# q and k as features by tokens, and a score order by row groups, in a two-layer decoder trunk

## The chip, the cores and the metric

The kernel runs on one core of a Trainium2 chip. Its time is the device time of one execution in microseconds. Before the change three runs gave a median of 648.08 us (648.01 to 648.24). The profile is one more execution of its own.

## The reference

Two layers for 256 tokens of width 1024, in float32. Layer 0 has block-sparse attention, which with one block of 256 keys is plain causal attention; layer 1 has differential attention, in which every head's 128 features are two halves of 64 with a softmax map each. Cut to what matters:

```python
for i in range(DEPTH):
    mod = (c_act @ ada_w[i] + ada_b[i])[:, None, :]          # c_act = silu(c)
    sh_a, sc_a, g_a, sh_f, sc_f, g_f = jnp.split(mod, 6, axis=-1)
    h = rms_norm(x, norm_g[i, 0]) * (1.0 + sc_a) + sh_a
    y = moba_attention(h, ...) if i % 2 == 0 else diff_attention(h, ...)
    x = x + g_a * rms_norm(y, norm_g[i, 1])
    h = rms_norm(x, norm_g[i, 2]) * (1.0 + sc_f) + sh_f
    x = x + g_f * rms_norm(swiglu(h, ffn_w_in[i], ffn_w_out[i]), norm_g[i, 3])

# attention: q, k, v = split(h @ w_qkv, 3); 8 heads
s = q k^T * scale + bias[head, bucket(q_pos - k_pos)];  s = where(rel >= 0, s, -1e30)
# layer 0: p = softmax(s);  o = p v
# layer 1: p[c] = softmax(s[c]) for the halves c = 0, 1;  o = (p[0] - lam * p[1]) v, then a norm per head
y = o @ w_o
```

## The kernel before

The 256 tokens are two tiles of 128. Every large product is written as three products in a faster 32-bit type (`R`): both operands are split into a high part (a copy by ScalarE, line 483 for weights, line 513 for activations) and a low part (a subtraction by VectorE, lines 484 and 514), and `mm` (line 485 on) adds high x high, high x low and low x high into one PSUM bank. In `mm` the activations `h` are the stationary operand, 128 features by 128 tokens, and a row block of weights with 512 columns is the moving one, so that a result has tokens on partitions and 512 features beside each other.

q and k are wanted with features on partitions. `qk_T` (line 574) therefore copies such a result to SBUF with ScalarE, turns it with four TensorE transposes (`pqk`) and copies it again. The scores (`softmax`, line 587) then take `qT` as stationary and `kT` as moving operand, head by head. In layer 1 each half of a head is a step of its own, with partitions 0 to 63 or 64 to 127 of both; the steps of the two halves stand in TensorE's queue where the plan puts them. A score of plain float32 counts as two products in the trace.

The relative-position bias is a table times a one-hot matrix (`build_bias`, line 318): a product with 8 rows, one per head, a copy to `bd` on 8 partitions, a store that repeats it 23 times in DRAM (`toep`), and loads with shifted rows (`load_bias`).

`first_block` is the start: norm of x, transposes of it (`ph`, `xT`), the adaLN vectors for the first feature chunk by one-column products on TensorE (`ada_first`, `pg` at line 419) and for the later chunks by VectorE multiply-adds (line 362) with sums over partitions by TensorE (line 374). Each chunk's shift and scale go to `hm`, `hq`, and to the projections of q and k. Ahead of it ten products of ones (`warm`, line 302), whose result nobody reads, run on TensorE.

The order of the work is not that of the code. Every step is an `op` with a cost, its buffers and a priority from the table `PRIORITIES`; `Schedule.run` plays the steps through with these costs, with PSUM and SBUF slots (`a` and `bc` have four PSUM banks each), and so writes the five queues (TensorE, VectorE, ScalarE, GpSimd, SyncE for transfers). On the chip each queue runs in that order.

Of the kernel before, what the change touches and what calls it, by code (L numbers as in the profile page):

```python
# [12 lines left out]
F = mybir.dt.float32  # L13
# [50 lines left out]
class Schedule:  # L64
# [35 lines left out]
    def run(self):  # L100
# [20 lines left out]
        order, act = [], "silu"  # L121
# [18 lines left out]
        while len(order) < len(ops):  # L140
            soon, moved = [], False
            for e in ENGINES:
# [25 lines left out]
                elif e == "PE":  # L168
# [6 lines left out]
                    cold -= d  # L175
# [52 lines left out]
def ld(nbytes):  # L228
    return nbytes / 360e3
# [3 lines left out]
def trunk_kernel(ctx: ExitStack, tc: tile.TileContext, x, c, rel_bias, ada_w, ada_b, norm_g, moba_w_qkv, moba_w_o,  # L233
# [51 lines left out]
    op("POOL", 0.05, lambda: nc.gpsimd.memset(mh.t, -0.5), w=[mh])  # L285
    op("DVE", 0.3, lambda: nc.vector.tensor_reduce(sel[:, 0], ident[:].rearrange("p (a b) -> p b a", a=4), AX.X, OP.add),
# [31 lines left out]
    def build_bias():  # L318
        oh = Buf("oh", "kT1", [NB + 1, NTOEP])
        tab = keep("tab", [NB + 1, H])  # L320
        bd = Buf("bd", "PT1", [H, NTOEP])
# [4 lines left out]
        op("PE", 0.65, lambda: nc.tensor.matmul(pb[:H, :NTOEP], tab.t[:], oh.t[:], start=True, stop=True), r=[tab, oh], w=[pb])  # L326
        op("DVE", 0.47, lambda: nc.vector.tensor_copy(bd.t, pb[:H, :NTOEP]), r=[pb], w=[bd])
        op("SP", 0.8, lambda: nc.sync.dma_start(toep.t, bd.t[:, None, :].to_broadcast([H, NCOPY, NTOEP])), r=[bd], w=[toep])

    def load_bias(g):  # L330
# [7 lines left out]
        for h in range(4):  # L338
            op("SP", ld(128 * 1024), lambda h=h: f(h), r=[toep], w=[(bt, K(h))])
# [58 lines left out]
    def ada_first(k0, n):  # L398
# [7 lines left out]
        for kc in range(0, KC, q):  # L406
# [3 lines left out]
            for j in range(2):  # L410
# [76 lines left out]
    def mm(ps, h, k, W, n, first, last, main=True):  # L487
# [6 lines left out]
        for q in range(3):  # L494
            op("PE", cost, lambda q=q: f(q), r=[(h, K(10 + k if q == 2 else k))] + [(b, K(1 if q == 1 else 0)) for b, _ in W],
               w=list(ps), main=main, name="mm" + W[0][0].name)

# [78 lines left out]
    def qk_T(st, l, t, g, w, ps):  # L576

        if t == 0:
# [7 lines left out]
            dst[:, :, t * 128:t * 128 + 128], p.t[:].rearrange("p (h q) -> p h q", h=4), AF.Copy), r=[p], w=[(dst, K(t))])  # L586

    def softmax(st, l, t, g):
# [358 lines left out]
```

## Time and profile before

| | us |
|---|---|
| median of the timed runs | 648.08 (648.01 to 648.24) |
| the profiled execution | 645.48 |
| its span, first to last instruction | 643.7 |
| TensorE busy | 627.5 (97%) |
| VectorE busy | 475.0 (74%) |
| ScalarE busy | 372.5 (58%) |

A product's duration in the trace is the time from its start to its end in a pipeline, longer than the distance to the next one: the mean of a 512-column product is some 390 to 410 ns, while 28 in a row take 6.35 us. What a product costs in a queue is therefore read from the time of a dense row of them. The chain of waits and the merged timeline give such rows.

### The profile page before, as it was taken

Reading aid. Unit: us, or ns where it says so; the run is one execution under the profiler, and the core shown is the slowest. Engines: PE = TensorE matmul, PEld = TensorE weight load, DVE = VectorE, ACT = ScalarE, POOL = GpSimd, SP = SyncE. Lnnn points to the kernel's source line nnn. Section 1 sums busy time; section 2 is a strip of 40 time slices with the busy share of each in tenths; the row PEclk is TensorE's granted clock in tenths of the full one; section 3 lists DMA queues with packets and bytes.
Section 4 is the critical chain, followed back from the end, with each engine's and each line's share of the span. In section 5 each row is a group of like instructions: output and inputs, shape, how many; then the busy total and the mean of one; then the engine's idle time right before and its main releaser. Section 6 shows DMA issues by size and latency. Waiting matters only on the chain.

```text
span 643.7 us, 8416 instructions
## 1 busy us (share of the span) xinstructions
PE 627.5 (97%) x2955; PEld 515.0 (80%) x2955; DVE 475.0 (74%) x602; ACT 372.5 (58%) x628; POOL 30.0 (5%) x66
## 2 busy tenths in 40 slices
PE   7899999999999999999989999999999999999996
PEld 6787878887888888888877777787788888888884
DVE  3798699987689969659885889898655657574633
ACT  6477697589364625345596777848655344453621
POOL 1000000031000000000021000211200000000001
PEclk9999999999999999999999999999999999999999
DMA  9999999997889987758965868472575587665301
GB/s 291 360 363 319 300 378 381 347 292 249 301 285 353 363 313 270 233 174 293 351 233 194 291 218 271 133 229 72 190 262 163 187 272 224 250 199 180 128 1 66
DMA packets 72487, 160.58 MB, mean 249 GB/s; under 512 B 5491, under 2 KB 22516, under 8 KB 72444
## 3 DMA queue, kind: packets, MB, share of 16 engines
q1 hardware_dynamic: 72252, 159.96, 73.0%
q8 instruction: 23, 0.38, 0.2%
q14 instruction: 20, 0.16, 0.1%
q10 hardware_dynamic: 192, 0.08, 0.0%
HBM read 158.69 MB, written 1.33 MB: 249 GB/s over the span
## 4 chain that ended last, share of the span: by engine, by line
PE 85%; DMA 5%; DVE 3%; ACT 3%; POOL 2%; issue 1%; SPq 1%; DVEq 0%; POOLq 0%; ACTq 0%
PE pf L492 19%; PE pg L492 16%; PE pu L492 16%; PE pq L492 10%; PE pv L492 6%; PE po L492 5%; PE pgu L492 3%; DMA bias<-toep 3%; PE ps L603 2%; PE pa L296 1%; PE po L649 1%; PE ph L296 1%; ACT hm L508 1%; DMA toep<-bd 1%; PE pg L419 1%
## 5 line engine op out<-in xcount | busy, mean ns | idle before, releaser
L492 PE MATMUL pg<-s_i,h 128*128 128x512 f32 x480 | 188.3, 392 | 0.0
L492 PE MATMUL pu<-s_i,h 128*128 128x512 f32 x480 | 187.1, 390 | 0.0
L484 DVE TENSOR_TENSOR s_i<-w_i,s_i 128x1024 fp32r<-128x1024 f32 (+1 forms) x96 | 107.0, 1133 | 50.7 <-ACT s_i L483 49.7
L492 PE MATMUL pf<-s_u,a 128*128 128x512 f32 x528 | 137.4, 392 | 0.0
L483 ACT ACTIVATE s_i<-w_i 128x1024 fp32r<-128x1024 f32 (+1 forms) x96 | 93.1, 989 | 73.3 <-PE pu L492 48.8
L492 PEld LDWEIGHTS pf<-s_u,a 128*128 128x128 f32 x528 | 97.9, 188 | 20.4 <-ACT s_u L483 0.4
L492 PEld LDWEIGHTS pg<-s_i,h 128*128 128x128 f32 x480 | 90.1, 188 | 18.8 <-DVE s_i L484 0.3
L492 PEld LDWEIGHTS pu<-s_i,h 128*128 128x128 f32 x480 | 90.1, 188 | 18.4
L362 DVE SCALAR_TENSOR_TENSOR acc<-aw,cact,acc 128x1024 f32<-128x1024 f32 x70 | 89.3, 1277 | 2.2 <-DMA aw<-in_ada_w_dram 1.8
L483 ACT ACTIVATE s_u<-w_u 128x1024 fp32r<-128x1024 f32 x44 | 46.4, 1059 | 58.3 <-PE pu L492 28.8
L484 DVE TENSOR_TENSOR s_u<-w_u,s_u 128x1024 fp32r<-128x1024 f32 x44 | 53.6, 1221 | 30.2 <-ACT s_u L483 29.8
L492 PE MATMUL po<-s_o,o 128*128 128x512 f32 x192 | 49.8, 399 | 0.0
L492 PE MATMUL pq<-s_q,h 128*128 128x512 f32 x192 | 47.7, 397 | 1.8 <-ACT h L513 1.8
L492 PEld LDWEIGHTS pq<-s_q,h 128*128 128x128 f32 x192 | 35.0, 188 | 10.5 <-ACT h L513 2.5
L484 DVE TENSOR_TENSOR s_q<-w_q,s_q 128x1024 fp32r<-128x1024 f32 x32 | 38.5, 1220 | 5.9 <-ACT s_q L483 5.6
L492 PEld LDWEIGHTS po<-s_o,o 128*128 128x128 f32 x192 | 34.9, 188 | 6.8 <-DVE o L665 0.4
L492 PE MATMUL pq<-s_q,hq 128*128 128x512 f32 x144 | 37.0, 408 | 2.5 <-ACT hq L513 2.5
L483 ACT ACTIVATE s_q<-w_q 128x1024 fp32r<-128x1024 f32 x32 | 33.3, 1054 | 4.8 <-PE pq L492 2.0
L492 PEld LDWEIGHTS pq<-s_q,hq 128*128 128x128 f32 x144 | 27.5, 195 | 9.2 <-ACT hq L513 3.0
L471 POOL TENSOR_SCALAR ms<-ss 128x1 f32<-128x1 f32 x16 | 7.3, 459 | 504.7 <-ACT z L542 497.9
L611 ACT ACTIVATE sx<-sx,mx 128x128 f32<-128x128 f32 (+1 forms) x48 | 21.3, 445 | 10.6 <-DVE mx L609 10.6
L492 PE MATMUL pgu<-s_i,h 128*128 128x512 f32 x96 | 26.1, 392 | 0.0
(141 smaller groups left out, 755.7 us busy)
## 6 DMA issues: line engine op xcount, KB each, us to landing
aw<-in_ada_w_dram SPq DMA_DIRECT2D x80, 512.0 KB
w_i<-in_ffn_w_in_dram SPq DMA_DIRECT2D x80, 512.0 KB
w_u<-in_ffn_w_out_dram SPq DMA_DIRECT2D x44, 512.0 KB
aw<-in_ada_w_dram SPq DMA_DIRECT2D x32, 256.0 KB
w_q<-in_moba_w_qkv_dram SPq DMA_DIRECT2D x16, 512.0 KB
w_q<-in_diff_w_qkv_dram SPq DMA_DIRECT2D x16, 512.0 KB
w_q0v<-in_moba_w_qkv_dram SPq DMA_DIRECT2D x8, 512.0 KB
w_o<-in_moba_w_o_dram SPq DMA_DIRECT2D x8, 512.0 KB
```

Of the source, the lines that this page charges most:

```text
L296: nc.tensor.transpose(dst[:, o:o + n], a, ident[:n, :n])
L362: op("DVE", tt(n) + 0.065, lambda: nc.vector.scalar_tensor_tensor(a.t, w(), cact[:, kc:kc + 1], a.t, op0=OP.mult, op1=OP.add), r=[cact, w. ...
L419: nc.tensor.matmul(pg[:, n * j + b:n * j + b + 1], w[:, e, j, b * 128:b * 128 + 128], cact[:, kc + e:kc + e + 1], start=kc + e + j + b == ...
L471: op("POOL", 0.16, lambda: nc.gpsimd.tensor_scalar(ms.t, m0.t[:], 1.0 / n, EPS, op0=OP.mult, op1=OP.add), r=[m0], w=[ms])
L483: op("ACT", ac(2 * n), lambda: nc.scalar.activation(b[:, 0], w.t[:], AF.Copy), r=[w], w=[(b, K(0))], name="hi" + name)
L484: op("DVE", tt(2 * n), lambda: nc.vector.tensor_sub(b[:, 1], w.t[:], b[:, 0].bitcast(F)), r=[w, (b, K(0))], w=[(b, K(1))], name="lo" + name)
L492: nc.tensor.matmul(p[:, :n], a, b[:, 1 if q == 1 else 0, s], start=first and q == 0, stop=last and q == 2)
L508: op("ACT", ac(128, 2, fps), lambda i=i, k=k: nc.scalar.activation(m[:, i], src[2](i), AF.Identity, bias=sh[:, k:k + 1], scale=G[:, k:k + 1]),
L603: nc.tensor.matmul(p[:, i * nk:i * nk + nk], qT[rows, h0 + i, t * 128:t * 128 + 128], kT[rows, h0 + i, 0:nk], start=True, stop=True)
L611: op("ACT", ac(nk, 2), lambda i=i, sx=sx, mx=mx, su=su: nc.scalar.activation(sx[:, i], sx[:, i], AF.Exp, bias=mx[:, i:i + 1], accum_out=su ...
L649: nc.tensor.matmul(p[:, i * 128:i * 128 + 128], a, b, start=kt == 0, stop=kt == t)
```

## The change

- In layer 0, and for heads 4 to 7 of layer 1, q and k are computed by `mmT` with the weights (128 x 128) as stationary and `h` of both tiles (256 columns) as moving operand. The result has features on partitions, and `qk_F` copies it once. For this the two tiles' activations lie in one SBUF tile `hh`. Heads 0 to 3 of layer 1 keep the old way.
- In layer 1 the scores of both halves are one step, in which the halves alternate.
- The bias product has 128 rows (16 copies of the 8 heads), and two stores take the table from 128 partitions.
- 22 instead of ten `warm` products, one more behind each of the four adaLN steps of the first chunk and five behind the last.
- A one-column silu right at the start, so that its table is loaded there.
- The planner's start without a loaded table, some of its costs, and the whole table of priorities are new, and so are all five queues.

```diff
-        order, act = [], "silu"
+        order, act = [], None
...
+    scr = keep("scr", [128, 1])
+    op("ACT", 0.2, lambda: nc.scalar.activation(scr.t, mh[:, 0:1], AF.Silu), r=[mh], w=[scr], act="silu")
...
-    for _ in range(10):
-        op("PE", 0.227, lambda: nc.tensor.matmul(warm.t[:].rearrange("p (a b) -> p a b", a=4), ones.t[:],
-                                                 ones.t[:, None, :].to_broadcast([128, 4, 128]), start=True, stop=True),
-           r=[ones], w=[warm], name="warm")
+    def heat(n, r):
+        def f():
+            nc.tensor.matmul(warm.t[:].rearrange("p (a b) -> p a b", a=4), ones.t[:],
+                             ones.t[:, None, :].to_broadcast([128, 4, 128]), start=True, stop=True)
+        for _ in range(n):
+            op("PE", 0.227, f, r=r, w=[warm], name="warm")
+    heat(22, [ones])
...
-        bd = Buf("bd", "PT1", [H, NTOEP])
+        bd = Buf("bd", "PT1", [128, NTOEP])
...
-        op("SP", 0.8, lambda: nc.sync.dma_start(toep.t, bd.t[:, None, :].to_broadcast([H, NCOPY, NTOEP])), r=[bd], w=[toep])
+        tc16 = Buf("tc16", "s2", [NB + 1, 128])
+        op("DVE", 0.2, lambda: nc.vector.tensor_copy(tc16.t[:].rearrange("p (c h) -> p c h", h=H), tab.t[:, None, :].to_broadcast([NB + 1, 16, H])),
+           r=[tab], w=[tc16])
+        op("PE", 0.65, lambda: nc.tensor.matmul(pb[:, :NTOEP], tc16.t[:], oh.t[:], start=True, stop=True), r=[tc16, oh], w=[pb])
...
+        op("SP", 0.6, lambda: store(0, 16), r=[bd], w=[(toep, K(0))])
+        op("SP", 0.3, lambda: store(16, NCOPY - 16), r=[bd], w=[(toep, K(1))])
...
-                    op("PE", 0.224 * len(es) * n, f, r=[cact, (w, K(j))], w=[pg], name="ada0")
+                    op("PE", 0.224 * len(es) * n, f, r=[cact, (w, K(j))], w=[pg], name="ada0", thin=True)
+                    heat(1, [ones, pg])
...
+        if not pe:
+            heat(5, [ones, pg])
...
+    def mmT(ps, h, k, W, first, last):
+        def f(q):
+            for p, (b, s, c) in zip(ps, W):
+                for j in range(2):
+                    nc.tensor.matmul(p[:, j * 256:j * 256 + 256].rearrange("p (t q) -> p t q", t=T),
+                                     b[:, 1 if q == 1 else 0, s, c + j * 128:c + j * 128 + 128], hh[:, :, 1 if q == 2 else 0, k],
+                                     start=first and q + j == 0, stop=last and q == 2, skip_group_check=True)
...
+    def qk_F(st, l, g, w, ps, hp):
...
+        op("ACT", ac(512, 0, True), lambda: nc.scalar.activation(
+            dst[:, 2 * hp:2 * hp + 2], ps.t[:].rearrange("p (h q) -> p h q", h=2), AF.Copy, scale=sc), r=[ps], w=[(dst, K(hp, 2 + hp))])
...
-                def f(p=p, rows=rows, h0=h0):
-                    for i in range(nh):
+            def f(pp=pp, h0=h0):
+                for i in range(nh):
+                    for m, p in enumerate(pp):
+                        rows = slice(0, 128) if l == 0 else slice(m * 64, m * 64 + 64)
                         nc.tensor.matmul(p[:, i * nk:i * nk + nk], qT[rows, h0 + i, t * 128:t * 128 + 128],
                                          kT[rows, h0 + i, 0:nk], start=True, stop=True)
...
-            for t in range(T):
-                qk_T(st, l, t, 1, "qT", ps[t][2])
-                qk_T(st, l, t, 0, "qT", ps[t][0])
-                qk_T(st, l, t, 0, "kT", ps[t][1])
+            for i, w, g in ((0, "qT", 0), (1, "kT", 0), (2, "qT", 1)):
+                for p in range(2):
+                    qk_F(st, l, g, w, ps[i][p], p)
...
+                        if g == 0:
+                            mm(ps, hT[t], k, W[k], 512, k == 0, k == KC - 1)
+                        else:
+                            mmT(ps, hT, k, [(*w, t * 256) for w in W[k]], k == 0, k == KC - 1)
...
 PRIORITIES = """
-od6sF00000IRFg+0{{vD001xmMF124D*!<NSO9MTh5(!ZvjD^Z&j7mt+W_+c(*f!L^8rEuBLQmxc>#z4y#c)esR73UDFXcgv;md@*#YeV`T;Kjg#sG_Zvv+R
+c>rVp000008~_CX9smOX000~SC;&bHFaSmXT>x|diU6SixB$)o-vH|X_5c9^4FMPdBLOr4KmkhuRsmuGZ2@=zn*lEYmI0~(J^`x%h5;b~vjM^Z&;bPkF#_=c
...
```

What this does to the queues is shown at three places. First TensorE at the start, before: `warm` are the products of ones, `pc` the transposes of c, the gains and the adaLN bias, `ph` those of the normed x, `pg` the one-column adaLN products, `pq` the first projections.

```order
L302 MATMUL warm<-ones 128x512 x10
L296 MATMUL pc<-ident,ng 128x64
L296 MATMUL pc<-ident,ab 128x96
L296 MATMUL pc<-ident,c_118 128x8
L296 MATMUL ph<-ident,xh 128x128 x8
L419 MATMUL pg_182<-cact,aw_125 128x1 x4
L296 MATMUL ph<-ident,xh 128x128 x8
L419 MATMUL pg_182<-cact,aw_125 128x1 x4
L419 MATMUL pg_182<-cact,aw_156 128x1 x8
L492 MATMUL pq_252<-s_q_191,hq_248 128x512
L492 MATMUL pq_256<-s_q_191,hq_250 128x512
```

And after; 15 `warm`, `pc` of the gains, 7 `warm`, `pc` of the adaLN bias and of c, and the first four `pg` stand ahead of these rows:

```order
L307 MATMUL warm<-ones 128x512
L436 MATMUL pg_168<-cact,aw_111 128x1 x4
L299 MATMUL ph<-ident,xh 128x128 x8
L307 MATMUL warm<-ones 128x512
L436 MATMUL pg_168<-cact,aw_142 128x1 x4
L307 MATMUL warm<-ones 128x512
L299 MATMUL ph<-ident,xh 128x128 x4
L436 MATMUL pg_168<-cact,aw_142 128x1 x4
L307 MATMUL warm<-ones 128x512 x4
L299 MATMUL ph<-ident,xh 128x128 x4
L307 MATMUL warm<-ones 128x512 x2
L526 MATMUL pq_264<-hh,s_q_178 128x256 x2
```

The adaLN products now come before and between the transposes of x, with a `warm` behind each group of four; the first projection product is one of 256 columns that reads `hh`.

Second the transfers at the start, SyncE's queue, before (`aw` are adaLN weights, `w_q` projection weights; `aw_125` and `aw_156` are those of the first feature chunk):

```order
L281 DMA x_68<-in_x_dram 128x1024
L411 DMA aw_105<-in_ada_w_dram 128x2x256
L281 DMA x_69<-in_x_dram 128x1024
L411 DMA aw_105<-in_ada_w_dram 128x2x256
L277 DMA c_118<-in_c_dram 8x128
L411 DMA aw_121<-in_ada_w_dram 128x2x256
L411 DMA aw_125<-in_ada_w_dram 128x4x128
L482 DMA w_q_130<-in_moba_w_qkv_dram 128x2x512
L411 DMA aw_125<-in_ada_w_dram 128x4x128
L482 DMA w_q_140<-in_moba_w_qkv_dram 128x2x512
L411 DMA aw_121<-in_ada_w_dram 128x2x256
L411 DMA aw_156<-in_ada_w_dram 128x4x128 x2
```

And after, where `aw_111` and `aw_142` are those of the first chunk:

```order
L281 DMA x_68<-in_x_dram 128x1024
L281 DMA x_69<-in_x_dram 128x1024
L428 DMA aw_111<-in_ada_w_dram 128x4x128
L277 DMA c_117<-in_c_dram 8x128
L502 DMA w_q_120<-in_moba_w_qkv_dram 128x2x512
L428 DMA aw_111<-in_ada_w_dram 128x4x128
L428 DMA aw_127<-in_ada_w_dram 128x2x256
L428 DMA aw_132<-in_ada_w_dram 128x2x256
L428 DMA aw_142<-in_ada_w_dram 128x4x128
L428 DMA aw_132<-in_ada_w_dram 128x2x256
L428 DMA aw_142<-in_ada_w_dram 128x4x128
L428 DMA aw_127<-in_ada_w_dram 128x2x256
```

The last transfer of the first chunk stands two places earlier, with one block of projection weights and one of adaLN weights fewer ahead of it.

Third the scores of layer 1 on TensorE, with buffer numbers, before: a piece from the scores of heads 4 to 7, for the second 128 queries (`ps` is a score bank; `ps_3642` belongs to the second half of the features, `ps_3646` to the first):

```order
L603 MATMUL ps_3642<-kT1_3497,qT1_3451 128x256 x2
L603 MATMUL ps_3646<-kT1_3497,qT1_3451 128x256 x2
L492 MATMUL pv0_3447<-s_q1v6_3405,h10_2994 128x512
L492 MATMUL pv1_3448<-s_q1v6_3405,h10_2994 128x512
L492 MATMUL pv0_3447<-s_q1v6_3405,h10_2994 128x512
L492 MATMUL pv1_3448<-s_q1v6_3405,h10_2994 128x512
L492 MATMUL pv0_3447<-s_q1v6_3405,h10_2994 128x512
L492 MATMUL pv1_3448<-s_q1v6_3405,h10_2994 128x512
L603 MATMUL ps_3662<-kT1_3497,qT1_3451 128x256 x2
L492 MATMUL pv0_3447<-s_q1v7_3513,h10_2994 128x512
L492 MATMUL pv1_3448<-s_q1v7_3513,h10_2994 128x512
```

And after, all scores of one group of heads, first those of the first 128 queries (`128x128`), then half of those of the second 128 queries; the two banks of each pair of rows belong to the two halves:

```order
L648 MATMUL ps_3772<-kT1_3651,qT1_3660 128x128
L648 MATMUL ps_3773<-kT1_3651,qT1_3660 128x128
L648 MATMUL ps_3772<-kT1_3651,qT1_3660 128x128
L648 MATMUL ps_3773<-kT1_3651,qT1_3660 128x128
L648 MATMUL ps_3772<-kT1_3651,qT1_3660 128x128
L648 MATMUL ps_3773<-kT1_3651,qT1_3660 128x128
L648 MATMUL ps_3772<-kT1_3651,qT1_3660 128x128
L648 MATMUL ps_3773<-kT1_3651,qT1_3660 128x128
L648 MATMUL ps_3789<-kT1_3651,qT1_3660 128x256
L648 MATMUL ps_3790<-kT1_3651,qT1_3660 128x256
L648 MATMUL ps_3789<-kT1_3651,qT1_3660 128x256
L648 MATMUL ps_3790<-kT1_3651,qT1_3660 128x256
```

Before, each bank was filled in one go; the banks of two halves were neighbours in some places, as in the first two rows, and in others a bank stood alone, as `ps_3662` behind six `pv` products. Now products into the two halves' banks alternate.

## Rows read from the trace of the kernel before

**Rows 1.** The page, part 1: busy time, share of the span, instructions.

```profile
PE 627.5 (97%) x2955; PEld 515.0 (80%) x2955; DVE 475.0 (74%) x602; ACT 372.5 (58%) x628; POOL 30.0 (5%) x66
```

**Rows 2.** Windows of 20 us: busy time, granted clock, DMA share, GB/s.

```profile
0.00:20.00 20.00, 16.08 (x61) 13.74 (x61) 7.82 (x17) 10.20 (x18) 2.83 (x16) 1.00 0.97 304
20.00:40.00 20.00, 18.04 (x80) 14.76 (x81) 18.02 (x32) 12.65 (x24) 0.00 (x0) 1.00 1.09 361
40.00:60.00 20.00, 20.00 (x93) 15.95 (x92) 18.46 (x31) 15.19 (x23) 0.00 (x0) 1.00 1.05 370
60.00:80.00 20.00, 20.00 (x107) 16.80 (x106) 11.89 (x13) 13.79 (x19) 0.00 (x0) 1.00 0.90 270
80.00:100.00 20.00, 19.05 (x93) 15.07 (x93) 18.62 (x25) 18.61 (x53) 0.00 (x0) 1.00 1.00 379
100.00:120.00 20.00, 20.00 (x118) 17.38 (x118) 19.81 (x26) 12.00 (x24) 0.00 (x0) 1.00 0.97 368
120.00:140.00 20.00, 20.00 (x112) 17.19 (x111) 18.37 (x25) 13.41 (x27) 3.17 (x7) 1.00 0.96 320
320.00:340.00 20.00, 18.12 (x83) 14.16 (x81) 17.43 (x24) 15.02 (x33) 5.91 (x12) 1.00 0.71 247
```

**Rows 3.** Chain of waits (first row of 40:46 alone): start, us, engine, tile, line, instructions.

```profile
42.61 0.79 PE pg L374 x8
...
110.51 1.78 PE po L649 x16
...
355.76 0.87 PE pqk L296 x8
...
358.46 1.09 PE ps L603 x8
...
360.13 1.08 PE ps L603 x8
...
368.29 1.06 PE ps L603 x4
...
370.01 1.92 PE ps L603 x8
...
387.55 1.64 PE ps L603 x16
...
399.91 1.07 PE ps L603 x8
...
627.25 6.35 PE pf L492 x28
```

**Rows 4.** Timeline, 0 to 30 us: start, us, engine, line, operation.

```profile
1.02 4.64 PE L302 MATMUL warm<-ones 128*128 128x512 f32 x10 [1.02 <-POOL ones L283]
...
14.36 5.12 PE L419 MATMUL pg<-cact,aw 128*128 128x1 f32 x24
...
20.03 0.88 ACT L508 ACTIVATE hm<-xT,scsh,scsh 128x128 f32<-128x128 f32 x2 [3.88 <-DVE scsh L354]
...
21.16 4.47 PE L492 MATMUL pq<-s_q,hq 128*128 128x512 f32 x12 [1.68 <-ACT hq L513]
```

**Rows 5.** TensorE's products by shape: busy us, mean ns, idle before.

```profile
L492 PE MATMUL pq<-s_q,h 128*128 128x512 f32 x192 | 47.7, 397 | 1.8 <-ACT h L513 1.8
L492 PE MATMUL pq<-s_q,hq 128*128 128x512 f32 x144 | 37.0, 408 | 2.5 <-ACT hq L513 2.5
...
L492 PE MATMUL pk<-s_q,hq 128*128 128x512 f32 x48 | 14.5, 411 | 0.0
...
L296 PE MATMUL pqk<-ident,qk 128*128 128x128 f32 x64 | 9.3, 275 | 0.5 <-ACT qk L583 0.5
```

**Rows 6.** Waits: engine, waited for, us in total, times, longest.

```profile
DVE sx L606 <- DMA bias<-toep: 3.4, 2, 2.6
```

More of the change, by code (lines that the diff above doesn't have):

```diff
@@ L338, in load_bias @@
         for h in range(4):
[L339 removed]
+            op("SP", 0.55, lambda h=h: f(h), r=[toep], w=[(bt, K(h))])
         return bt
@@ L496, in mm @@
                w=list(ps), main=main, name="mm" + W[0][0].name)
+    hh = const.tile([128, T, 2, KC, 128], R, name="hh")
+    def mmT(ps, h, k, W, first, last):
[5 more added lines that the diff above has]
+                                     start=first and q + j == 0, stop=last and q == 2, skip_group_check=True)
+        for q in range(3):
+            op("PE", 2 * len(ps) * 0.12, lambda q=q: f(q), r=[(h[t], K(10 + k if q == 2 else k)) for t in range(T)] +
+               [(b, K(1 if q == 1 else 0)) for b, _, _ in W], w=list(ps), main=True, name="mm" + W[0][0].name)
     def new_h(t, name):
@@ L686, in first_block @@
         h = [new_h(t, f"hq{t}") for t in range(T)]
-        ps = [[Buf("pq0", "a"), Buf("pq1", "a"), Buf("pq2", "bc")] for t in range(T)]
+        ps = [[Buf(f"pq{i}{p}", "a" if i < 2 else "bc") for p in range(2)] for i in range(3)]
         W2 = []
@@ L697, in first_block @@
                 modulate(h[t], (xT[t], KR(k0 // 4, (k0 + n - 1) // 4 - k0 // 4 + 1), lambda i, t=t, k0=k0: xT[t][:, k0 + i]), 0, 0, k0, n, False)
[L698 to L703 removed]
+            for k in ks:
+                mmT(ps[0] + ps[1], h, k, [(W[k - k0][s][0], s, c) for s in range(2) for c in (0, 256)], k == 0, k == KC - 1)
+            for k in ks:
+                mmT(ps[2], h, k, [(*W2[k], c) for c in (0, 256)], k == 0, k == KC - 1)
         return h, ps
@@ L710, in trunk_kernel @@
             build_bias()
-            for t in range(T):
-                qk_T(st, l, t, 1, "qT", ps[t][2])
-                qk_T(st, l, t, 0, "qT", ps[t][0])
-                qk_T(st, l, t, 0, "kT", ps[t][1])
-            W = []
-            for t in range(T):
-                p = Buf("pk1", "a")
-                for k in range(KC):
-                    if t == 0 and k % 2 == 0:
-                        W.extend(qk1(0, k, D + 512, 2))
-                    mm([p], hT[t], k, [W[k]], 512, k == 0, k == KC - 1)
-                qk_T(st, l, t, 1, "kT", p)
-                softmax(st, l, t, 0)
+            for i, w, g in ((0, "qT", 0), (1, "kT", 0), (2, "qT", 1)):
+                for p in range(2):
+                    qk_F(st, l, g, w, ps[i][p], p)
+            W, ps = [], [Buf("pk1", "a") for _ in range(2)]
+            softmax(st, l, 0, 0)
+            for k in range(KC):
+                if k % 2 == 0:
+                    W.extend(qk1(0, k, D + 512, 2))
+                mmT(ps, hT, k, [(*W[k], c) for c in (0, 256)], k == 0, k == KC - 1)
+            for p in range(2):
+                qk_F(st, l, 1, "kT", ps[p], p)
+            softmax(st, l, 1, 0)
         else:
@@ L839, in trunk_kernel @@
         for b in o.bufs:
-            if b.cls and b.t is None:
+            if b.cls in ("h0", "h1"):
+                b.t = hh[:, int(b.cls[1])]
+            elif b.cls and b.t is None:
                 b.t = pools.get(b.cls, sb).tile(list(b.shape), b.dt, name=b.name, tag=f"{b.cls}_{b.slot}")
```

165 lines of the change are left out of this document (84 added, 81 removed).

## The prediction

> **What bounds the kernel now.** I read the page first, then the table of 20 us windows, the groups of TensorE's products by shape, the chain of waits and the first 30 us of the timeline. TensorE is busy for 97% of the span [rows 1]. From 40 us on the windows show it full or nearly so, with VectorE next: 18.6, 19.8 and 18.4 of 20 us between 80 and 140 us, while the DMA share there is 0.96 to 1.00 [rows 2]. So from about 21 us to the end the kernel costs what TensorE's queue costs, and anything that shortens that queue shortens the run, unless VectorE or the transfers cannot follow in the first 140 us.
>
> A 512-column product costs 6.35/28 = 0.227 us in a dense stretch [rows 3]. At 2.4 GHz the columns alone are 512/2.4 = 0.2133 us, so 0.0135 us comes on top of each product, whatever it is made of.
>
> The start is different. The window 0 to 20 us prints a granted clock of 1.00 like the rest [rows 2], but no change of level is recorded in it, and the spacing tells another story: ten throw-away products take 4.64 us, 0.46 each [rows 4], against 512/1.2 = 0.427 at the lower of the two levels. 24 one-column products of the adaLN vectors take 5.12 us, 0.213 each [rows 4]; eight of them later take 0.79, 0.099 each [rows 3]. The first twelve projection products take 4.47 us where 12 x 0.227 = 2.72 would do [rows 4]. So all of TensorE's work before about 24 us ran at 1.2 GHz, and this work is on the path: the adaLN products end at 19.48, VectorE makes shift and scale, ScalarE makes `hm` at 20.03, and the first projection product starts at 21.16 [rows 4].
>
> **The change part by part.** All sums are against the profiled execution (645.48 us, of which 643.7 span); the median of the timed runs, 648.08, is 2.6 above it, and I subtract the gain from that median.
>
> (a) *The start.* Twelve more throw-away products stand ahead of the first transposes, nine more among and behind the adaLN products, and the transfers of the first adaLN chunk come earlier. Before, the chunk's last transfer is behind 2 x 512 KB of x, 8 x 256 KB of adaLN weights and 2 x 512 KB of projection weights, 4.2 MB (the sizes follow from the shapes in the order); now behind 3.4 MB. The first window moves 304 GB/s [rows 2], 6.1 MB in 20 us; with nothing landing in the first 2 us that is 0.34 MB/us, so 4.2 MB are there at 14.4 us and 3.4 MB at 12.1. Before, TensorE was then still 5 us behind, because 24 products at 0.213 were left from 14.36 on. If the higher level is on by then, eight one-column products are left after the last landing, 8 x 0.099 = 0.8, so they end at about 13; one transfer more (256 KB, 0.8 us) is ahead of the `a` step that ScalarE now has before `hm`. With the old 21.16 - 19.48 = 1.7 us from the last adaLN product to the first projection, the latter starts at about 15.5: 5.7 us earlier. Bounds: 2 us (the later transfers' pace) to 8 us (nothing but the 1.7 us after 11.5).
> The early silu table takes a 1.28 us load from between c and `cact`; that is inside this number, as is the 0.2 us tile that triggers it. The nine later throw-away products (2.0 us at 0.227) stand where TensorE waits for transfers or for `hm`, which is 1.7 us alone; they cost nothing as long as that wait is there, and at most 2.0 us.
>
> (b) *The level.* If the first projection products run at 2.4 GHz, 4.47 - 2.72 = 1.75 us goes. Did the old ten products show that more of them will do it? After these 4.64 us no rise came; inside the first twelve projection products one did, since 4.47 us is short of 12 x 0.427 = 5.12 [rows 4]. 22 products at the lower level are 22 x 0.427 = 9.4 us, twice the stretch without a rise and twice the one with it, so I take it that the level rises inside them. After that it has to hold through transposes and one-column products; ahead of the second layer TensorE pauses for 1.8 us [rows 5] in a window that still shows 1.00 [rows 2].
>
> (c) *Transposes gone.* q and k of layer 0 and of the second half of layer 1 come out as features by tokens: 48 of the 64 transposes (`pqk`) go, and twelve ScalarE copies. Eight in a row take 0.87 us, 0.109 each [rows 3]: 48 x 0.109 = 5.2 us less.
>
> (d) *Half-length products.* 144 + 48 products of layer 0 and 96 of the 192 of layer 1 [rows 5], 288 of 512 columns, become 576 of 256. No row has a 256-column product of this type. The nearest rows: 0.227 for 512 columns, and the values-times-probabilities products, 16 of 128 fp32 columns in 1.78 us, 0.111 each with a weight load for every one [rows 3]. Eight one-column products, which are little but their loads, take 0.099 each [rows 3]; so a load and a 128-column product must run beside each other to fit into 0.111. A load thus fits under 256 columns as well, and I take 256/2.4 + 0.0135 = 0.120 us: 576 x 0.120 - 288 x 0.227 = +3.8 us. Below, 0.111 each would give -1.4; above, a load that is not hidden gives 0.219 (the fourth rival).
> The Trainium skill ("TensorE: Matmul & The Clock Gate", Back-to-back issue gap) has N/2.4 + 2.5 ns for a warm product. By it the half products would be 0.109 us and this term -2.6, the forecast 631.3. The 512-column row says otherwise: 13.5 ns on top, not 2.5, so I keep 0.120.
>
> (e) *Scores of layer 1.* Twelve pieces of scores stand in TensorE's queue before, one for each half of the 128 features of a head. For the second 128 queries a piece alone takes 1.06 us (four of these); two pieces of the same half in a row 1.92; two pieces of different halves in a row 1.07 [rows 3]. So pieces of different halves already run side by side where they happen to be neighbours. Now each pair is one step, its products alternating: 4 x 1.07 = 4.28 instead of 4 x 1.06 + 1.92 + 1.07 = 7.23, 2.95 less. For the first 128 queries: before 1.09 + 1.08 (alone) and 1.64 (two neighbours of different halves) [rows 3]; a pair now is at most 1.64 and at least half of 2.17, 1.09; I take 1.3, so 3.81 - 2.6 = 1.2 less. Together 4.1 less.
>
> (f) *The bias table* is stored from 128 partitions instead of 8, and earlier; its store and loads lie beside projection products, and the loads keep their number. I cost it at nothing; VectorE waited 3.4 us in all for the bias [rows 6], which would be the most that it gives back, if TensorE waited behind that.
>
> Sum: -5.7 - 1.75 - 5.2 + 3.8 - 4.1 = -12.95. The first two, 7.45 us, have to survive the first 140 us, where VectorE has 0.2 us of slack in 100 to 120 and transfers run at a share of 0.97 [rows 2]. VectorE's work is not reduced (its casts and multiply-adds are the same): 105.2 us in the six windows from 20 to 140 us, with 8.1 of the 14.8 us of slack in 60 to 80 alone [rows 2]; ending 8 us earlier would need 94% of it throughout. I let 2.5 us be lost there: a gain of 10.4, **637.7 us**.
>
> **The rivals.** *Second: the start's gain is swallowed.* The first projection block is paced by transfers (shares 1.09 and 1.05 from 20 to 60 us) and VectorE (18.0 and 18.5 of 20) [rows 2], so that an earlier first product only waits longer for the second chunk. Against it: the old block had TensorE full from 40 us on. Then only c, d and e are left: -5.5, 642.6 us.
> *Third: the level does not rise, or falls again.* Then 22 products take 9.4 us, `cact` waits for none of them but the transposes of c do; 9 more cost 0.427 each; 32 one-column products and 16 transposes at 0.213 are 10.2 us as before. The first projection would start at about 1.3 + 9.4 + 1 + 3.8 + 10.2 + 1.7 = 27.4 us, 6.2 later than before; with -5.5 from the rest, 648.8. Against it is the argument of (b).
> *Fourth, slower: loads are not hidden behind half products.* Each product needs its own weight load, and a load alone is worth 0.099 us (one-column products [rows 3]). Serial, a half product costs 0.120 + 0.099 = 0.219: 576 x 0.099 = +57, and the run takes 695 us. It decides from 0.018 us more on each (10.4/576), that is from 0.138 us. The row of 0.111 with a load in each speaks against it, but that is another type of product, and it is the step on which most instructions hang.
> The Trainium skill (same page, Part 3, The mechanism) lets a weight load overlap a running product only when their row groups differ. By that rule the fourth rival would hold for all 576, 695 us; the rows of 0.111 do not agree with it.
> *Fifth: a new order opens new waits.* All five queues were planned anew, and no row says which stall a plan will meet; if it gives back 5 to 13 us, the run lands between 643 and 651.
>
> **How the numbers follow.** Forecast 0.60, with a range of its own of 632 to 643; second 0.17; third 0.05; fourth 0.10; fifth 0.08. What a measurement of this kernel can tell from no change is 0.2%, 1.3 us. Faster: 0.60 + 0.17 + 0.05 of the fifth = 0.82; same: most of the third and 0.03 of the fifth, 0.07; slower: the fourth and what is left, 0.11. Above the forecast the range goes to the fifth rival's middle; below, to term (d) at the lower bound with nothing lost, 648.1 - 18: 630 to 646.5.
>
> **What would show it.** The first projection product near 15.5 us, and twelve times two of them at 0.12 us each; a spacing of 0.227 among the throw-away products before 10 us; the half products' spacing in a dense stretch, 0.120 (right) or over 0.138 (wrong); 16 `pqk` transposes left; layer 1's pairs of scores at 1.07 and 1.3 us; VectorE above 94% between 15 and 130 us. I am wrong if TensorE shows new idle time in the first 60 us, or if the windows of the second layer's attention are no shorter.

## The result and the profile after

The changed kernel takes 643.98 us (median of 6 runs, 641.58 to 645.85), the kernel before 648.05 (646.84 to 648.50): ratio 0.9935, interval 0.9912 to 0.9959. A second comparison (e0_after below) gave 0.9965 (0.9951 to 0.9978), 644.43 against 646.51. So it is faster by 2 to 4 us, where 10.4 were forecast; the time lies in the range, the size is wrong. The profiled execution of one experiment (e3_hh32) took 885 us at a granted clock of at most 0.65, so only that experiment's other times are read.

The profiled execution took 644.03 us, its span 642.1. TensorE is busier than before in time, though 48 transposes went [rows 1]:

```profile
PE 630.3 (98%) x3216; PEld 524.7 (82%) x3216; DVE 474.2 (74%) x603; ACT 366.7 (57%) x616; POOL 31.1 (5%) x66
```

Three groups of rows tell why. First the dense stretches. In what follows, the distance of a product is the time from its start to the start of the next one. This is the last dense stretch in the chain of waits of the changed kernel (start, us, engine, tile, line, instructions), which answers to the last row of [rows 3]:

```profile
628.54 7.46 PE pf L512 x32
```

7.46/32 is 0.233 us for a 512-column product, where it was 6.35/28 = 0.227. The change doesn't rewrite these products; those of `pg` and `pu` only read their activations from `hh` now. The groups by shape (busy us, mean ns of one) show it for all of them. In the trace of before `pg`, `pu` and `pf` stand at 392, 390 and 392 ns:

```profile
L492 PE MATMUL pg<-s_i,h 128*128 128x512 f32 x480 | 188.3, 392 | 0.0
L492 PE MATMUL pu<-s_i,h 128*128 128x512 f32 x480 | 187.1, 390 | 0.0
L492 PE MATMUL pf<-s_u,a 128*128 128x512 f32 x528 | 137.4, 392 | 0.0
```

In the changed kernel they stand at 397, 395 and 397. The last two groups are the half products and the transposes that are left; [rows 5] has those of before:

```profile
L512 PE MATMUL pg<-s_i,hh 128*128 128x512 f32 x480 | 190.6, 397 | 0.1
L512 PE MATMUL pu<-s_i,hh 128*128 128x512 f32 x480 | 189.6, 395 | 0.0
L512 PE MATMUL pf<-s_u,a 128*128 128x512 f32 x528 | 140.5, 397 | 0.0
L526 PE MATMUL pq<-hh,s_q 128*128 128x256 f32 x480 | 61.5, 285 | 0.7 <-ACT hh L548 0.7
...
L299 PE MATMUL pqk<-ident,qk 128*128 128x128 f32 x16 | 2.3, 274 | 0.0
```

Second the start, TensorE in the timeline:

```profile
1.57 5.77 PE L307 MATMUL warm<-ones 128*128 128x512 f32 x15 [1.57 <-POOL tab L331]
...
10.17 1.05 PE L436 MATMUL pg<-cact,aw 128*128 128x1 f32 x8 [0.56 <-ACT cact L317]
...
13.79 1.70 PE L436 MATMUL pg<-cact,aw 128*128 128x1 f32 x8
...
16.77 1.71 PE L436 MATMUL pg<-cact,aw 128*128 128x1 f32 x8
...
21.89 4.03 PE L526 MATMUL pq<-hh,s_q 128*128 128x256 f32 x28
```

The first half product starts at 21.89 us; before, the first product started at 21.16 [rows 4]. The first eight adaLN products take 1.05 us, but the third and the fourth 1.70 and 1.71, 0.213 each, as before. Windows of 2 us (PE, PEld, DVE, ACT, POOL busy, then granted clock, where 1.00 is the 2.4 GHz level and 0.50 the 1.2 GHz one, DMA share, GB/s) tell what happened:

```profile
6.00:8.00 2.00, 2.00 (x9) 1.38 (x8) 0.22 (x1) 0.92 (x4) 0.83 (x3) 1.00 1.00 303
8.00:10.00 2.00, 1.61 (x8) 1.04 (x7) 0.35 (x2) 0.06 (x1) 0.11 (x1) 1.00 1.07 334
10.00:12.00 2.00, 1.83 (x16) 1.79 (x16) 0.99 (x3) 1.67 (x4) 0.93 (x3) 1.00 1.13 361
12.00:14.00 2.00, 2.00 (x15) 1.91 (x15) 1.73 (x3) 1.00 (x2) 0.00 (x0) 0.71 1.10 379
14.00:16.00 2.00, 2.00 (x9) 1.82 (x10) 0.00 (x0) 0.19 (x1) 0.00 (x0) 0.50 1.11 358
...
22.00:24.00 2.00, 2.00 (x15) 2.00 (x14) 1.89 (x4) 2.00 (x3) 0.00 (x0) 0.73 1.10 350
24.00:26.00 2.00, 2.00 (x20) 2.00 (x19) 1.72 (x3) 0.38 (x1) 0.00 (x0) 1.00 1.08 345
```

The upper level came early: the profile's record of the clock has it at 6.03 us, and seven throw-away products behind it take 1.7 us, where 7 x 0.427 = 3.0 is the lower level. Then come short waits (1.61 of 2 us busy at 8 to 10) and mostly one-column products, and at 12.86 the level falls, to come back at 23.1, about where the kernel before had its only rise, 24.3.

Third layer 1, in the chain: the scores, and a dense row of half products (256 columns), 4.70/40 = 0.118 us each.

```profile
354.87 1.09 PE ps L648 x16
...
370.26 1.93 PE ps L648 x16
...
377.55 4.70 PE pq L526 x40
...
389.73 1.96 PE ps L648 x24
...
396.98 1.06 PE ps L648 x8
```

The scores take 6.04 us in all, where the trace of before has 11.03 (7.22 + 3.81, distances of starts summed by kind).

Cutting both traces where the same work starts or ends gives the balance, in us. The last column is the experiment e4_phase below, in which the unchanged products are back at 227 ns:

| stretch (starts of TensorE's products) | before | after | e4_phase |
|---|---|---|---|
| to the first projection product | 21.16 | 21.89 | 21.92 |
| to the last product of k, layer 0 (`pk`) | 58.88 | 54.54 | 55.49 |
| to the first feed-forward product, layer 0 (`pg`) | 59.80 | 63.05 | 61.46 |
| to the last one (`pf`) | 188.80 | 192.84 | 188.96 |
| to the first of layer 1 (`pu`) | 120.11 | 110.46 | 109.91 |
| to the last (`pf`) | 188.33 | 192.82 | 188.94 |
| sum | 637.08 | 635.60 | 626.68 |

The two feed-forward stretches, whose products the change doesn't rewrite, lost 8.5 us together (4.04 and 4.49).

### The profile page after: what moved, and what is told of

The parts are those of the page before. It is cut to its first block, busy times and chain, and to the rows that moved or that the text cites. A ratio compares the mean times of both kernels' runs of the same rounds, so it can differ in the third digit from the quotient of the medians.

```text
span 642.1 us, 8916 instructions
## 1 busy us (share of the span) xinstructions
PE 630.3 (98%) x3216; PEld 524.7 (82%) x3216; DVE 474.2 (74%) x603; ACT 366.7 (57%) x616; POOL 31.1 (5%) x66
## 4 chain that ended last, share of the span: by engine, by line
PE 82%; DMA 5%; DVE 5%; ACT 3%; issue 2%; POOL 1%; DVEq 0%; POOLq 0%; SPq 0%; ACTq 0%
PE pf L512 18%; PE pu L512 17%; PE pg L512 17%; PE po L512 5%; PE pv L512 5%; DMA bias<-toep 4%; PE pq L526 4%; PE pgu L512 3%; PE pq L512 2%; PE warm L307 2%; PE po L696 2%; PE pa L299 1%; DVE a L379 1%; ACT s_q L503 1%; DVE s_q L504 1%
## 5 line engine op out<-in xcount | busy, mean ns | idle before, releaser
L512 PE MATMUL pg<-s_i,hh 128*128 128x512 f32 x480 | 190.6, 397 | 0.1
L512 PE MATMUL pu<-s_i,hh 128*128 128x512 f32 x480 | 189.6, 395 | 0.0
L512 PEld LDWEIGHTS pg<-s_i,hh 128*128 128x128 f32 x480 | 90.1, 188 | 21.9 <-ACT hh L548 0.5
L512 PEld LDWEIGHTS pu<-s_i,hh 128*128 128x128 f32 x480 | 90.2, 188 | 21.2
L526 PE MATMUL pq<-hh,s_q 128*128 128x256 f32 x480 | 61.5, 285 | 0.7 <-ACT hh L548 0.7
L526 PEld LDWEIGHTS pq<-hh,s_q 128*128 128x128 f32 x480 | 59.3, 190 | 2.8 <-issue 0.9
L512 PE MATMUL po<-s_o,hh 128*128 128x512 f32 x192 | 50.3, 403 | 0.0
L512 PEld LDWEIGHTS po<-s_o,hh 128*128 128x128 f32 x192 | 35.0, 188 | 7.2
L512 PE MATMUL pgu<-s_i,hh 128*128 128x512 f32 x96 | 26.5, 398 | 0.0
L512 PE MATMUL pv<-s_q0v,hh 128*128 128x512 f32 x96 | 24.9, 401 | 0.9 <-ACT s_q0v L503 0.9
```

The source lines that it names most:

```text
L512: nc.tensor.matmul(p[:, :n], a, b[:, 1 if q == 1 else 0, s], start=first and q == 0, stop=last and q == 2)
L526: nc.tensor.matmul(p[:, j * 256:j * 256 + 256].rearrange("p (t q) -> p t q", t=T), b[:, 1 if q == 1 else 0, s, c + j * 128:c + j * 128 + 1 ...
```

## The experiments

Theory A: the new one-column tile `scr` takes 32 bytes among the constants, and so the weight tiles behind it in SBUF start 32 bytes past a multiple of 64; this makes the 512-column products slower. Rivals: it was that execution alone (B), or other engines' traffic in the new order (C).

**e0_after**: the changed kernel again.

> The changed kernel once more, beside the kernel before on the same chip. Theory A (addresses): the 4-byte tile for the early silu takes 32 bytes of SBUF and puts the weight tiles behind it at addresses that are 32 past a multiple of 64; a 512-column product that streams from there takes 232 ns instead of 227. Then this run shows 231 to 233 ns again in dense stretches, and a time near 644 us. Theory B (chance): the spacing of 232 belonged to that one execution or chip; then it may read 227 here, and the time would be some 633. Theory C (traffic): the new order puts other engines' SBUF traffic beside the products; then 232 and 644, as by A.

Measured: 644.43 us, and distances of 231 to 233 ns on average, as in the first execution. B is out.

**e1_aligned**: 32 bytes less ahead of the weight tiles.

```diff
-        e, nl, sg = keep("le", [128, 2]), keep("nlam", [128, 1]), keep("sg", [128, 128])
+        le, sg = keep("le", [128, 3]), keep("sg", [128, 128])
+        e, nl = Buf("le", t=le.t[:, 0:2]), Buf("nlam", t=le.t[:, 2:3])
```

> As the changed kernel, with the same order of instructions; a 4-byte constant shares a tile with another one, which takes 32 bytes out ahead of the weight tiles, so that these start at multiples of 64 as before the change. A: 512-column products back at 226.5 to 228 ns; 2,064 of them times 5.4 ns are 11 us, so 633 us. B and C: no change from the changed kernel, 644 us and 232 ns.

Measured: 638.83 us, ratio 0.9876 (0.9856 to 0.9896). Addresses alone, with the same order, give 5.6 us: C is out as the whole cause. But only half of A's 11 us came, and the distance is 230, not 227.

**e2_bshift**: the kernel before, 32 bytes further.

```diff
+    const.tile([128, 8], F, name="pad")
     order = S_.best()
```

> The kernel before with one unused 32-byte tile behind its constants, nothing else. A: all 2,352 products of 512 columns go from 227 to 232 ns, 12.7 us more: 661 us, ratio 1.020. B and C: 648 us, ratio 1.00.

Measured: 648.22 us, ratio 1.0015 (0.9999 to 1.0031), distances as before. The groups are within a nanosecond of those of before:

```profile
L492 PE MATMUL pg<-s_i,h 128*128 128x512 f32 x480 | 188.3, 392 | 0.0
L492 PE MATMUL pu<-s_i,h 128*128 128x512 f32 x480 | 187.1, 390 | 0.0
L492 PE MATMUL pf<-s_u,a 128*128 128x512 f32 x528 | 137.4, 393 | 0.0
```

So A is wrong: tiles 32 past a multiple of 64 cost nothing when all are.

**e3_hh32**: as e1_aligned, the tile `hh` moved by 32 bytes (it changes places with `scr`).

```diff
+    hh = const.tile([128, T, 2, KC, 128], R, name="hh")
     scr = keep("scr", [128, 1])
...
-    hh = const.tile([128, T, 2, KC, 128], R, name="hh")
```

> As e1_aligned, but the tile hh of the activations starts 32 past a multiple of 64, and the weight tiles at multiples of 64. If only the address of the moving operand counts: 512-column products at 227 ns as in e1_aligned, half products (which stream hh) between 119 and 122 ns, so 0 to 1.6 us above e1_aligned. If the stationary operand's address counts as well: the 1,536 products with hh as stationary at 232 ns and those of pf at 227, some 8 us above e1_aligned.

Measured: 644.17 us, ratio 0.9947 (0.9926 to 0.9967), 5.3 us above e1_aligned. By its time, the stationary operand's address counts as well, though less than the 8 us written.

What is common to these? I sorted the distances of consecutive 512-column products by how far, modulo 128 bytes, the address that a product streams from lies from the address of the stationary operand that is loaded beside it (the next product's). Mean ns (count), distances under 250 ns, from 30 us on:

| run | 0 apart | 64 apart | 32 or 96 apart |
|---|---|---|---|
| before | 227.7 (2142) | 229.2 (14) | |
| e2_bshift | 227.8 (2139) | 230 (1) | 233 (15) |
| after | 231.5 (234) | 231.7 (120) | 233.2 (1580) |
| e1_aligned | 230.9 (368) | 230.0 (1426) | 233.2 (140) |

In the kernel before nearly everything was 0 apart. Where single products 0 apart stand among others, they stay slow (231.5, 230.9); also before, the first four behind a stop take 231 on average, and only from the twelfth on 98% of them take 226.7. That is theory E, relative address. It was tested by making everything 0 apart in the changed kernel, and by spoiling the kernel before.

**e4_phase**: as e1_aligned, with small tiles in a pool of their own and `hh` where its remainder is that of the weight tiles.

```diff
     sb = ctx.enter_context(tc.tile_pool(name="sb", bufs=1))
+    smp = ctx.enter_context(tc.tile_pool(name="smp", bufs=1))
...
+    hh = const.tile([128, T, 2, KC, 128], R, name="hh")
     sel = keep("sel", [128, 4, 32])
...
+    pools["sm"] = smp
```

> As e1_aligned (same order of instructions), but now all weight tiles, the tile hh and the other stationary tiles start at addresses with the same remainder modulo 128. Theory E (relative address): a 512-column product takes 226.7 ns in a steady row if the moving operand and the next product's stationary operand have the same remainder modulo 128, 230 if they are 64 apart, 233 if 32 or 96 apart. Then dense stretches read 226 to 227 ns as before the change, and the 512-column products together take 10 us less than in the changed kernel: 634 us on this chip's scale (where the kernel before has 646.5 and the changed one 644.4). Rival (theory A kept: multiples of 64 are enough): no change from e1_aligned, 639 us. Rival (traffic of the new order): 644 us.

Measured: 635.45 us, ratio 0.9822 (0.9804 to 0.9840), where 634 was written. 1,919 products 0 apart take 227.7 on average. The groups are back at 392 and 390 ns:

```profile
L514 PE MATMUL pg<-s_i,hh 128*128 128x512 f32 x480 | 188.3, 392 | 0.1
L514 PE MATMUL pu<-s_i,hh 128*128 128x512 f32 x480 | 187.1, 390 | 0.0
```

The row of half products and the last feed-forward row in its chain give 4.78/40 = 0.120 and 7.30/32 = 0.228 us:

```profile
373.07 4.78 PE pq L527 x40
...
619.79 7.30 PE pf L514 x32
```

**e5_bh32**: the kernel before, activation tiles 32 bytes further.

```diff
+    hp = ctx.enter_context(tc.tile_pool(name="hp", bufs=1))
...
+    hp.tile([128, 8], F, name="pad")
+    pools.update(h0=hp, h1=hp)
```

> The kernel before, with its activation tiles (the stationary operand of q, k, v, the output projection and the first feed-forward product) 32 bytes further, weight tiles where they were. Theory E: 1,822 of the 2,352 products of 512 columns have operands 32 apart, 5.7 ns more each, 10.4 us: 657 us, ratio 1.016; the last feed-forward product (pf) stays at 227 ns. Rivals: no change, 646.5 us.

Measured: 656.82 us, ratio 1.0152 (1.0130 to 1.0174): 10 us, as written. In its chain of waits a projection row and the last feed-forward row stand side by side:

```profile
391.87 3.73 PE pq L493 x16
...
639.04 6.36 PE pf L493 x28
```

3.73/16 = 0.233 with the moved tile, 6.36/28 = 0.227 without it. 1,649 products 32 or 96 apart take 233.1. So theory E holds in both directions, with one limit: all products 0 apart were 0 or 256 apart modulo 512, and none in any run was 128 apart modulo 256. Whether 128 is as good as 256 isn't shown.

The next kernels ask about the start. Theory F: it was lost to the clock's fall at 12.9 us. G: an earlier start is swallowed by transfers and VectorE (the prediction's second rival).

**e6_heat**: four throw-away products behind each adaLN step.

```diff
-                    heat(1, [ones, pg])
+                    heat(1, [ones, pg], 4)
```

> As e4_phase, with four throw-away products instead of one behind each of the four adaLN steps of the first chunk. Theory F: the start lost its gain because TensorE's clock fell back at 12.9 us, after a stretch of one-column products and short waits. With more columns in between it stays at the upper level; then the first half product comes at about 17.5 us instead of 21.9 and the run takes 630 us. Rival G (the earlier start is swallowed by transfers and VectorE): the first product comes earlier, but the last product of k of layer 0 (pk) at 76 us as before, and the run takes 634 us. Rival H (the level falls all the same): the first product at 25 us, 637 us.

Measured: 635.30 us, ratio 0.9821 (0.9795 to 0.9847), no change. The level falls all the same at 13.8 us, but is back at 17.2. The throw-away products that came with it use up what that saves, and the first half product comes later, at 22.45 us where e4_phase has 21.92:

```profile
19.84 1.87 PE L310 MATMUL warm<-ones 128*128 128x512 f32 x7
...
22.45 3.51 PE L528 MATMUL pq<-hh,s_q 128*128 128x256 f32 x28
```

**e8_hold2, e8_hold3**: more of them, also where TensorE waits (`burn(n)` writes n throw-away products; four short ones behind the bias product aren't shown).

```diff
     transposes(pc, K(0), [(0, lambda: c8.t[:])], [c8])
+    S_.ops[-1].fn = lambda f=S_.ops[-1].fn: (f(), burn(3))
...
-                    heat(1, [ones, pg])
+                    heat(1, [ones, pg], 2)      # 3 in e8_hold3
...
+            if hot and i == off:
+                S_.ops[-1].fn = lambda f=S_.ops[-1].fn: (burn(hot, lambda: pg[:, 128:512], 3), f())
```

> As e4_phase, with throw-away products where TensorE waits at the start: three behind the transpose of c, two instead of one behind each adaLN step of the first chunk, three ahead of the second chunk's sums and four short ones behind the bias product. Theory F (the start is lost to the lower level of TensorE's clock between 12 and 32 us): the granted clock stays at 1.0 from about 7 us on; then the first half product is at 18.5 us as in the one execution of e7_inturn that had the upper level until 24 us, pk ends at 73 us instead of 77.4, and the run takes 631.5 us, 4 below e4_phase. Rival G (transfers and VectorE pace the block): the level holds, and pk still ends at 77 us, 635 us. Rival H: the level falls all the same, 635 to 637 us.

> As e8_hold2 with three throw-away products behind each adaLN step. F: if two are not enough to hold the level and three are, this run alone shows 1.0 from 7 us on and 632 us (0.9 us of more products); if both hold, 0.5 to 0.9 us above e8_hold2. G and H as there.

Measured: 634.27 us, ratio 0.9805 (0.9789 to 0.9822), and 633.32, ratio 0.9792 (0.9773 to 0.9810). In e8_hold3 the level is the upper one from 5.0 us to the end; the first half product is at 19.09, 2.8 us earlier than in e4_phase, and the end of `pk` at 76.55, only 0.9 earlier. The windows (columns as above) show TensorE waiting between 40 and 60 us, where the changed kernel's is full (10.00 of 10 in both):

```profile
20.00:30.00 10.00, 9.89 (x71) 8.51 (x69) 9.79 (x18) 4.41 (x9) 0.00 (x0) 1.00 1.00 305
...
40.00:50.00 10.00, 9.40 (x78) 9.12 (x77) 9.72 (x19) 5.68 (x10) 0.00 (x0) 1.00 1.09 363
50.00:60.00 10.00, 9.68 (x79) 9.28 (x78) 8.04 (x16) 7.08 (x11) 0.00 (x0) 1.00 1.02 371
```

and the timeline what for: weights that ScalarE converts when their transfer lands, at a DMA share of 1.09.

```profile
47.77 3.13 PE L534 MATMUL pq<-hh,s_q 128*128 128x256 f32 x24 [0.60 <-ACT hh L556]
...
48.99 1.06 ACT L512 ACTIVATE s_q<-w_q 128x1024 fp32r<-128x1024 f32 x1 [1.27 <-DMA w_q<-in_moba_w_qkv_dram]
...
56.26 3.91 ACT L512 ACTIVATE s_q<-w_q 128x1024 fp32r<-128x1024 f32 x4 [1.29 <-DMA w_q<-in_moba_w_qkv_dram]
...
57.37 2.84 PE L534 MATMUL pq<-hh,s_q 128*128 128x256 f32 x19 [0.27 <-ACT s_q L512]
```

But in this execution the transfers moved 305 GB/s between 20 and 30 us, in e8_hold2 358, so that some of these waits may belong to this execution. In e8_hold2 the level is low twice more after the start, from 25.3 to 28.7 us and from 134.5 to 138.0:

```profile
18.06 3.51 PE L534 MATMUL pq<-hh,s_q 128*128 128x256 f32 x28
...
20.00:30.00 10.00, 9.78 (x61) 8.70 (x60) 9.82 (x18) 4.11 (x9) 0.00 (x0) 0.83 1.09 358
...
135.09 3.41 PE L521 MATMUL po<-s_o,hh 128*128 128x512 f32 x8
```

Its first half product comes 3.9 us earlier than that of e4_phase, and its `pk` ends at 74.61, still 2.8 earlier; 1.9 are left at 133.8. The eight products at 135.09 then take 3.41 us at the lower level, 2.09 in e4_phase, and 0.5 is left at the first feed-forward product. Against e4_phase (0.9822, and 0.9813 when run again) the gain of both runs is 0 to 2 us and not told apart by the intervals.

So F is right about the clock: with the upper level, the first half product comes 2.8 to 3.9 us earlier. That the added products keep the level up is seen in the mean granted clock of all executions, 0.995 to 0.999 in the four of e8_hold3 and 0.986 to 0.993 in the eight of e4_phase and e4_again; one trace couldn't show it, as e7_inturn below held the level to 24.3 us without them. G is right in part: of the earlier start 0.9 to 2.8 us reach the end of `pk`.

**e9_thin**: the nine throw-away products among the adaLN steps with one column.

```diff
+            if thin:
+                nc.tensor.matmul(warm.t[:, 0:1], ident.t[:], ones1.t[:], start=True, stop=True)
+                return
```

> As e4_phase, but the nine throw-away products among and behind the adaLN steps have one column instead of 512; the 22 ahead of them stay. If these nine do nothing for the level, they cost only their time at the lower level, 0.427 us each, of which those ahead of the last adaLN step count: the first half product comes 1.5 us earlier, at 20.4 us, and the run takes 634 us. If they help to hold the level, the first half product comes no earlier and the time is the same or 1 us more.

Measured: 635.46 us, ratio 0.9818 (0.9800 to 0.9836), no change. The profiled execution, the slowest of the six, took 638.68. In it the first half product is at 21.48, 0.4 us earlier, but the upper level returns at 26.7 instead of 22.0 and is lost once more from 139.3 to 142.7, and the first half products run slower:

```profile
21.48 5.88 PE L530 MATMUL pq<-hh,s_q 128*128 128x256 f32 x28
```

In e4_phase they take 3.54:

```profile
21.92 3.54 PE L527 MATMUL pq<-hh,s_q 128*128 128x256 f32 x28
```

By the median times, the nine products pay for themselves and no more; that they bring the level back earlier rests on one trace without them and two with them.

**e4_again**: e4_phase once more.

> e4_phase once more, for comparison on the same chip: ratio 0.982 to the kernel before. As the order is the same, the granted clock may rise and fall at other moments of the first 35 us than in the first execution; by F the first half product and the end of pk then move with it, by up to 4 us.

Measured: 634.81 us, ratio 0.9813 (0.9791 to 0.9835). Here the clock rose and fell at the same moments as in e4_phase, within 0.1 us.

**e7_inturn**: scores one half after the other.

```diff
-                for i in range(nh):
-                    for m, p in enumerate(pp):
-                        rows = slice(0, 128) if l == 0 else slice(m * 64, m * 64 + 64)
+                for m, p in enumerate(pp):
+                    rows = slice(0, 128) if l == 0 else slice(m * 64, m * 64 + 64)
+                    for i in range(nh):
```

> As e4_phase, but in layer 1 a pair of score pieces is issued one half after the other instead of alternating. By the rows of before (two pieces of different halves in a row took 1.07 us together) they run side by side anyway: within 0.7 us of e4_phase. Rival (the products run in the order in which they are written, so only alternating ones run side by side): the four pairs of the second 128 queries take 2.1 us instead of 1.07, those of the first 128 some 0.5 more each: 5 us above e4_phase.

Measured: 634.47 us, ratio 0.9815 (0.9800 to 0.9829), no difference that can be told. In the chain the scores are 7.24 us instead of 6.04:

```profile
348.26 1.64 PE ps L650 x16
...
364.13 2.03 PE ps L650 x16
...
383.86 2.50 PE ps L650 x22
...
391.59 1.07 PE ps L650 x8
```

So neighbours of different halves run side by side in either order, and alternating saves 1.2 us more. The start has the same queue as e4_phase and shows that the clock's moments differ between executions: in this execution the level held from 7.3 to 24.3 us and was low for 6.8 us after that (columns as above).

```profile
10.00:20.00 10.00, 9.44 (x73) 8.64 (x73) 6.47 (x15) 6.64 (x14) 0.94 (x3) 1.00 1.10 343
20.00:30.00 10.00, 9.17 (x48) 7.66 (x47) 9.82 (x18) 4.25 (x9) 0.00 (x0) 0.72 1.08 358
30.00:40.00 10.00, 10.00 (x81) 10.00 (x81) 7.93 (x14) 6.89 (x11) 0.00 (x0) 0.94 1.09 356
```

The first half product is then at 18.25, 3.7 us before that of e4_phase; at the end of `pk` 1.7 us are left, part of it lost to the later fall.

## Why the prediction was wrong

The step that failed first stands in the part on what bounds the kernel: "so 0.0135 us comes on top of each product, whatever it is made of". It depends on where the operands lie. The change adds a tile of 32 bytes and moves `hh` among the constants. I costed the time of the operation that writes the tile ("inside this number") and put its place in SBUF at nothing, and some 1,900 unchanged products went from 227.7 to 233 ns. Summed over the 512-column products that is 10.1 us between the changed kernel and e4_phase; the half products are 1.3 us faster in the changed kernel, half of that in the first 30 us where the clock's moments differ, so 8.8 us remain, all of the difference between the two profiled executions (644.03 and 635.24). No rival held it: the fifth (new waits) has the right time, 643 to 651, by another mechanism. That 643.98 lies inside the stated range is luck in the same way; its upper end, too, is not quite what it says, since the fifth rival's middle is 647 and not 646.5.

Without that, e4_phase's balance is -10.4 us, the number forecast, but this is luck, since the terms came out otherwise:

- (a), the start, failed: -5.7 became +0.8. That the level rises inside 22 throw-away products was right (6.03 us). "After that it has to hold through transposes and one-column products" was the condition, and it didn't hold. The second rival was right in part: of a start 2.8 us earlier 0.9 reached the end of `pk` in e8_hold3, of one 3.9 earlier 2.8 in e8_hold2. Nor was 15.5 us in reach; the earliest first half product of any run is at 18.06, and at the upper level (e7_inturn) TensorE's own work, 32 one-column products, transposes and throw-away products, ends at 16.3 us, not at the 13 that I took from the transfers.
- (b) came in part: the first 28 half products take 3.54 us in e4_phase, but a second fall of the level, from 28.8 to 32.2 us, takes about as much back (3.4 us at half the pace, 1.7).
- (c) was right: 16 `pqk` are left.
- (d) was right in size: with operands 0 apart the half products' median distance is 120 ns, the value taken; loads are hidden, and the fourth rival is out: 536 half products, each with a load of its own and all on the full array, follow each other at 120 ns. With that, the sentence that a load overlaps a running product only when the row groups differ (the Trainium skill, "TensorE: Matmul & The Clock Gate", Part 3, The mechanism) does not agree. The same section of the Trainium skill also lets a load into the background weight buffer go ahead of running products, which would fit. The 2.5 ns on top of the columns that the Trainium skill gives for a warm product by itself (same page, Back-to-back issue gap), 109 ns for 256, do not agree with the 120 either.
- (e) was right in mechanism and 0.9 too small: 5.0 us instead of 4.1.
- (f) was nearly right. VectorE waited 4.7 us for the bias, 3.4 before [rows 6]. In the chain of waits the bias lands at 88.73 us, later than before (86.24); VectorE and ScalarE go on from there to `ppt`, for which TensorE waits 0.9 us, as it did not before:

```profile
DVE sx L653 <- DMA bias<-toep: 4.7, 3, 1.8
...
PE ppt L299 <- ACT sx L667: 0.9, 1, 0.9
```

- The layer-1 stretch gained 10.2 us, where (c), (d) and (e) forecast 4.6 for it and brought 6.1. Another 3.0 are the transposes of the normed rows: 24 of them lay in this stretch before, with the wait of 1.8 us behind eight of them [rows 5], 4.41 us in all; in e4_phase 16, 1.45 us, as the other eight stand ahead of it. The rest, 1.1, is spread over products that waited less. I had priced new waits of the new order and no old ones that go.
- The 2.5 us given back in 80 to 140 us didn't show: the stretch from `pk` to the first `pg` is 1.7 us longer in e4_phase, but ten products of v (2.3 us) moved into it.

What stays open: why products 32 bytes apart are slower, and whether a product's own weights or the next one's count. Nearly all have the same remainder here; in the changed kernel 60 products with only the next one's 32 apart take 233.5, and 54 with only their own 231.0, but in e5_bh32 81 of the latter kind take 233.0. One thing the runs do say: at the 1.2 GHz level nothing comes on top of the columns, whatever the addresses. There 512-column products are 427 ns apart, which is 512/1.2, both with operands 32 apart (ten at the start of e5_bh32) and 0 apart (seven at the start of e2_bshift).

## What to carry to other kernels

When a change adds or moves a tile, compare the dense rows of products that it doesn't touch before adding up those it does: 5 ns on 1,900 of them took 8.9 of the 10.4 us that the same queues gain in e4_phase. For products of this type keep the tiles that TensorE streams and those it loads a multiple of 256 bytes apart, with small tiles in a pool of their own. An early start is worth what the first block leaves of it, 0.9 to 2.8 us of 2.8 to 3.9 here, and a clock raised early need not stay up: read its record and not only the first rise.

## What the runs showed that I had not expected

- A 512-column product of this type takes 226.7 ns in a steady row at the upper level if its operands are 0 apart modulo 128 bytes (0 modulo 256 in all runs); on average 227.7, against 230.0 (64 apart) and 233.2 (32 or 96 apart). Moving all tiles together by 32 bytes changes nothing (ratio 1.0015), moving the activations alone costs 1.5%.
- The half products go the other way, a little: 117 ns median 64 apart, 118 ns 32 or 96 apart, 120 together.
- The same queue can meet the clock's levels at other moments: e7_inturn, whose start is that of e4_phase, held the upper one from 7.3 to 24.3 us, e4_phase from 4.9 to 11.8. The first half product moved by 3.7 us with it, the profiled execution by 0.9.
- e8_hold3, at 633.32 us, is 2.1% faster than the kernel before and e4_phase 1.8%, where the changed kernel, which has the same queues as e4_phase and differs in addresses alone, is 0.35 and 0.65% faster.
